# DMA row length of the first load in a streaming row-sum kernel

## The chip, the cores and the metric

The kernel runs on one core of a Trainium2 chip. The metric is device time in microseconds of one execution.

## The reference

```python
# x: (32, 512, 1024) float32, multiplier: 0.5
def reference(x, multiplier):
    return (np.sum(x, axis=-1) * multiplier).astype(np.float32)
```

There are 16384 rows of 1024 numbers, 67.1 MB to read and 65.5 KB to write. Each number is used once.

## The kernel before

The 16384 rows are cut into eight blocks of 128 partitions x 16 rows. Seven blocks are whole loads of 8.39 MB into three rotating buffers; in HBM, the 16 rows of one partition lie one after another, so a partition's part of a block is one run of 64 KiB. The vector engine (DVE) sums each block with one instruction; of block 6 the scalar engine (ACT) takes half. The last block comes in five pieces, so that little work is left when the last byte has landed.

```python
    x_pool = ctx.enter_context(tc.tile_pool(name="x", bufs=3))
    # ... cut ...
    for b in range(n_blocks - 1):
        c0 = b * B                                   # B = 16
        t = x_pool.tile([P, B, D], fp32, name="xb")  # 128 x 16 x 1024
        loads.append(nc.sync.dma_start(out=t, in_=x_rows[:, c0 : c0 + B, :]))
        h = B if b < n_blocks - 2 else B // 2
        nc.vector.reduce_sum(
            out=sums[:, c0 : c0 + h], in_=t[:, 0:h, :], axis=mybir.AxisListType.X
        )
        # ... multiply by 0.5 into res; half of block 6 goes to the scalar engine ...
    # ... last block: loads of 8, 5 and 2 rows, then the last row in two parts ...
    # ... two stores of the results ...
    # at build time, loads that wait for nothing are moved to the program's entry
```

## Time and profile before

| what | before | where from |
|---|---|---|
| time | 162.17 us (161.99 to 162.18) | three runs |
| span of the profiled run | 160.2 us | page, first line |
| DMA packets | 2016, 97.4% of 16 engines' span | page, part 3 |
| DVE busy | 74% | page, part 1 |
| first block seen by DVE | 21.78 us | timeline |
| one further whole load | 19.33 to 19.35 us | distance between the starts of two reductions |

"Seen" is the moment at which DVE begins on a block, some 0.02 us after the last of the 16 engines has reported its part landed. A load is spread over 16 DMA engines, and each moves 8 partitions of it. Since DVE starts each block only when it has landed, the distance between two starts is the time that the DMA engines took for one load. The lines themselves stand in the prediction below.

### The profile page before, as it was taken

What the parts mean: (1) busy time and instruction counts of PE and PEld (TensorE: products, weight loads), DVE (VectorE), ACT (ScalarE), POOL (GpSimd) and SP (SyncE); (2) the same over time, 40 slices, a digit from 0 to 9 for tenths busy, and PEclk for the clock granted to TensorE, in tenths of its full rate; (3) what the DMA queues carried; (4) which work ended last, traced back from release to release, by engine and by line L of the source; (5) the groups of instructions that cost most, each with busy time, mean ns of one, the idle gap of its engine ahead of it and who ended that gap; (6) DMA issues with size and microseconds to landing.
All of it is one profiled execution on the core that took longest, in us unless ns stands there. A gap on an engine that the chain in (4) does not pass through costs nothing.

```text
span 160.2 us, 138 instructions
## 1 busy us (share of the span) xinstructions
DVE 119.3 (74%) x34; ACT 17.3 (11%) x31; POOL 0.2 (0%) x4
## 2 busy tenths in 40 slices
DVE  0000059997799969999599995999959999597443
ACT  0000000000000000000000000000000000599952
POOL 0000000000000000000000000000000000000000
DMA  7996996996996996997997998979969969999992
GB/s 278 507 524 262 524 524 262 524 524 262 524 524 262 524 524 262 524 475 311 524 442 344 524 409 376 524 311 475 524 278 507 524 278 507 393 393 425 430 399 72
DMA packets 2016, 67.18 MB, mean 419 GB/s; under 512 B 480, under 2 KB 608, under 8 KB 736
## 3 DMA queue, kind: packets, MB, share of 16 engines
q1 hardware_dynamic: 2016, 67.18, 97.4%
HBM read 67.11 MB, written 0.07 MB: 419 GB/s over the span
## 4 chain that ended last, share of the span: by engine, by line
DMA 75%; DVE 22%; SPq 1%; issue 0%; DVEq 0%
DMA xb<-in_x_dram 75%; DVE sums L96 22%; SPq L114 1%; DVE xb L80 0%; SPq L120 0%; SPq L94 0%; DVE res L99 0%; DVEq L205 0%
## 5 line engine op out<-in xcount | busy, mean ns | idle before, releaser
L96 DVE TENSOR_REDUCE sums<-xb 128x16 f32<-128x16384 f32 (+1 forms) x7 | 112.0, 16001 | 33.3 <-DMA xb<-in_x_dram 33.3
L70 ACT ACT_TABLE_LOAD x1 | 1.3, 1283 | 137.9 <-DMA xb<-in_x_dram 137.9
L70 ACT ACTIVATE xb<-xb 128x1024 f32<-128x1024 f32 x15 | 15.7, 1045 | 2.1 <-DMA xb<-in_x_dram 2.1
L80 DVE CUSTOM_DVE_ANT_0 xb<-xb 128x512 f32<-128x512 f32 (+1 forms) x9 | 5.6, 664 | 5.0 <-DMA xb<-in_x_dram 5.0
L70 ACT ACTIVATION_READ_ACCUMULATOR xb<-xb 128x1 f32 x15 | 2.8, 187 | 0.0
L99 DVE TENSOR_SCALAR res<-sums 128x16 f32<-128x16 f32 (+1 forms) x7 | 1.2, 174 | 0.2
L80 DVE DVE_READ_ACCUMULATOR2_ANT res<- 128x1 f32 x9 | 0.7, 83 | 0.0
L80 DVE CUSTOM_DVE_ANT_0 xb<-xb,part 128x224 f32<-128x224 f32 x1 | 0.5, 450 | 0.2 <-DMA xb<-in_x_dram 0.2
L191 POOL MEMSET const-bfloat16-1.0<- 128x1 bf16 x1 | 0.1, 101 | 0.0
L191 POOL MEMSET const-uint8-127<- 128x1 uint8 x1 | 0.1, 101 | 0.0
L191 POOL MEMSET const-float32-0.0<- 128x1 f32 x1 | 0.1, 98 | 0.2 <-issue 0.2
L191 POOL MEMSET const-float32-1.0<- 128x1 f32 x1 | 0.1, 98 | 0.0
L80 DVE DVE_READ_ACCUMULATOR2_ANT part<- 128x1 f32 x1 | 0.1, 83 | 0.0
## 6 DMA issues: line engine op xcount, KB each, us to landing
xb<-in_x_dram SPq DMA_DIRECT2D x1, 4096.0 KB, 31.1
xb<-in_x_dram SPq DMA_DIRECT2D x1, 2560.0 KB, 36.9
xb<-in_x_dram SPq DMA_DIRECT2D x1, 1024.0 KB, 38.9
xb<-in_x_dram SPq DMA_DIRECT2D x1, 288.0 KB, 39.1
xb<-in_x_dram SPq DMA_DIRECT2D x1, 224.0 KB, 39.2
xb<-in_x_dram SPq DMA_DIRECT2D x7, 40.8
out_dram<-res SPq DMA_DIRECT2D x1, 56.0 KB, 10.0
out_dram<-res SPq DMA_DIRECT2D x1, 8.0 KB, 1.4
```

The costliest lines, as they stand in the source:

```text
L70: acts.append(nc.scalar.activation(out=t[:, r, :], in_=t[:, r, :], func=mybir.ActivationFunctionType.Copy, scale=mul, accum_out=res[:, col ...
L80: return nc.vector.tensor_tensor_reduce(out=t[:, r, lo:mid], in0=t[:, r, lo:mid], in1=t[:, r, mid:hi], scale=mul, scalar=start, op0=ADD, o ...
L96: nc.vector.reduce_sum(out=sums[:, c0 : c0 + h], in_=t[:, 0:h, :], axis=mybir.AxisListType.X)
L99: nc.vector.tensor_single_scalar(out=res[:, c0 : c0 + h], in_=sums[:, c0 : c0 + h], scalar=mul, op=mybir.AluOpType.mult,)
L114: nc.sync.dma_start(out=t[:, lo:hi, :], in_=x_last[:, lo:hi, :])
L191: nc = _bacc.Bacc("TRN2", target_bir_lowering=False, num_devices=1)
```

## The change

A DMA is cut into packets of one contiguous run each, here 64 KiB at most. The change caps the run at 8 KiB for the first block alone, so that its 128 packets become 1024. Its intent is to have the first, cold load run in shorter units, so that all engines come up to speed sooner; bytes, addresses, buffers and order stay.

```diff
-        loads.append(nc.sync.dma_start(out=t, in_=x_rows[:, c0 : c0 + B, :]))
+        loads.append(
+            nc.sync.dma_start(
+                out=t,
+                in_=x_rows[:, c0 : c0 + B, :],
+                max_dma_last_dim=65536 if b else 8192,
+            )
+        )
```

The first load's pattern goes from 128 x 16384 elements to 128 x 8 x 2048, one dimension more. Nothing else differs.

## The prediction

> **What bounds the kernel now.** I read the first page for the load of each engine and of the DMA queue, then the chain of waits in order of time, then the timeline for the moments at which each load was seen, and last a table of stretches cut at exactly those moments. The page and the chain first:
>
> ```profile
> DVE 119.3 (74%) x34; ACT 17.3 (11%) x31; POOL 0.2 (0%) x4
> q1 hardware_dynamic: 2016, 67.18, 97.4%
> DMA 75%; DVE 22%; SPq 1%; issue 0%; DVEq 0%
> ```
>
> The reader is to see one queue whose packets fill 97.4% of the time of 16 DMA engines, beside a vector engine (DVE) that is busy 74%. The chain puts 22% on DVE, and that needs care. It gets there because a load into one of three buffers waits for the reduction that frees the buffer. Here is where it does so (start, length, what):
>
> ```profile
> 0.43 40.66 DMA xb<-in_x_dram
> 41.09 0.02 issue
> 41.11 17.23 DVE sums L96
> 58.34 0.02 issue
> 58.36 40.78 DMA xb<-in_x_dram
> ```
>
> A load issued at 58.36 us takes 40.78 us to land because an earlier load is still draining in front of it in the queue. One whole load takes about 19.3 us, so the queue holds work for some 21 us when the buffer comes free: the link through DVE has that much slack, and the true chain is the queue alone. The table of stretches tests this. Its columns are the stretch, its length, busy time of each engine, the clock, the mean share of the DMA engines and GB/s:
>
> ```profile
> 0.00:21.78 21.78, 0.00 (x1) 0.00 (x0) 0.20 (x4) 1.00 1.02 433
> 21.78:41.11 19.33, 17.39 (x2) 0.00 (x0) 0.00 (x0) 1.00 1.00 434
> 41.11:137.87 96.76, 86.98 (x11) 0.00 (x0) 0.00 (x0) 1.00 0.99 428
> 137.87:147.58 9.71, 8.86 (x3) 9.64 (x17) 0.00 (x0) 1.00 0.97 418
> 147.58:153.68 6.10, 2.54 (x8) 4.34 (x9) 0.00 (x0) 1.00 0.99 424
> 153.68:156.18 2.50, 1.93 (x7) 2.19 (x5) 0.00 (x0) 1.00 0.97 398
> ```
>
> Each edge is the moment at which a consumer starts on a freshly landed load, so each length is the time of one load (the third: of five). From 21.78 us on, the DMA share is 0.97 to 1.00, and the rate is flat at about 430 GB/s. The kernel is bound by the DMA engines' own rate from about 2 us to about 157.5 us. DVE has 1.9 us idle ahead of each block, as the timeline says of the second:
>
> ```profile
> 21.78 17.22 DVE L96 TENSOR_REDUCE sums<-xb 128x16 f32<-128x16384 f32 x1 [21.78 <-DMA xb<-in_x_dram]
> 41.11 17.22 DVE L96 TENSOR_REDUCE sums<-xb 128x16 f32<-128x16384 f32 x1 [1.91 <-DMA xb<-in_x_dram]
> ```
>
> So whatever delays the DMA engines anywhere delays the end by the same amount. Nothing later in the queue absorbs it.
>
> **What the Trainium skill says.** (1) "DMA: Bandwidth & Descriptors", section "Where 436 GB/s comes from", gives a ceiling of 435.2 GB/s for the 16 ports. The 434 GB/s of a whole 64 KiB-row load says that it is reached: no row size can make a load appreciably faster. (2) The same page, "Why small descriptors are slow (HBM only)", names a fixed cost for each packet of about 3 cycles inside the DMA engine, and a fetch of 32 bytes of descriptor data. Three cycles at the 850 MHz of section (1) would be 3.5 ns. The trace agrees that there is a fixed cost but shows a larger one, 10 to 12 ns with all that goes with it (below); I use the trace's. (3) The same page, "Why a DMA increments its semaphore by 16 and not by 1": the number of engines is set by the slowest dimension. It is 128 partitions before and after, so all 16 engines stay in use, with an eighth of the partitions' bytes each. The trace before moves 434 GB/s, which needs all 16. (4) "Perfetto Trace Analysis", section "DMA Instruction — HWDGE (DVE, Sync)": an engine may begin to consume descriptors before all of them have been generated. No view of the kernel before can show this for 1024 descriptors, since all of its DMAs have 128 data packets each.
>
> **The change part by part.** Bytes, addresses, buffers, waits and the order of instructions stay as they are; only the first load is cut into 128 x 8 packets of 8 KiB where it had 128 of 64 KiB.
>
> Removed: 128 packets of 64 KiB, 8 for each engine. One takes 19.33 / 8 = 2.416 us.
>
> Added: 1024 packets of 8 KiB, 64 for each engine. The kernel already has loads with shorter rows, and each is also 8 packets for each engine. The stretches of its last block give their cost: 32 KiB rows (8 rows of x) 9.71 / 8 = 1.214 us, 20 KiB rows 6.10 / 8 = 0.763 us, 8 KiB rows 2.50 / 8 = 0.3125 us. At the 64 KiB rate they would be 1.208, 0.755 and 0.302. The excess of a packet over a share of a long one is therefore (2 x 1.214 - 2.416) / 1 = 12 ns from the first, (3.2 x 0.763 - 2.416) / 2.2 = 11 ns from the second, (8 x 0.3125 - 2.416) / 7 = 12 ns from the third. It contains the completion packets of these loads, of which the changed load has no more than before, and edges read to 0.01 us, so I take 8 to 11 ns. Each engine gets 64 - 8 = 56 more packets: 56 x 8 to 11 ns = 0.45 to 0.62 us, middle 0.53 us. All of it lies on the path.
>
> Start-up, the uncertain term: the first load is seen at 21.78 us, of which 8 x 2.416 = 19.33 us is transfer at full rate and 2.45 us is start. In the window of the first 3.2 us of the trace, the 16 first packets (one for each engine) have a share of 90.0%:
>
> ```profile
> DMA packets 16, 1.05 MB, mean 328 GB/s; under 512 B 0, under 2 KB 0, under 8 KB 0
> q1 hardware_dynamic: 16, 1.05, 90.0%
> ```
>
> That is 0.900 x 3.2 = 2.88 us for each packet, 0.46 us more than later ones. Shorter packets could cut this, or move it. Against that stands the making of eight times as many descriptors. The closing store bounds its speed: all 144 of its packets (128 and 16 completions) begin within 5 slices of 0.055 us, 0.275 us, so at most 1.9 ns for each. The new load needs 1024 + 16: at most 2.0 us. If they are made engine by engine, the last engine could begin up to 15/16 of 2.0 = 1.9 us after the first; today's first packets are spread over about 0.9 us (slices of the first 3 us). The worst case of this step is thus an estimate of +1.0 us; if engines are served in turn or the present 0.9 us has another cause that overlaps, 0. I put +0.1 us on start-up as a whole, between -0.4 and +1.0.
>
> Moved: the first reduction starts 0.5 to 0.6 us later, so the fourth load is issued that much later, still about 20 us before the queue would run dry. DVE's, ACT's and the store's work doesn't change. The issuing queue may take longer over the first instruction (0.38 us now); the second load has some 20 us to be ready, so this is hidden.
>
> Sum: 0.53 + 0.1 = +0.6 us; 162.17 + 0.6 = about 162.8, which I shade to **162.7 us** since the packet cost is more likely at its lower end.
>
> **The rivals.**
> *A faster start.* Packets of 8 KiB let writes finish earlier and might recover the 0.46 us stretch of the first packets. For it: the stretch is real. Against it: the last engine to start sets when the load is complete, and a stretch caused by 16 engines beginning at once on cold memory wouldn't ask for the packet size. It would make about 162.2 us, a net of nothing.
> *Descriptors become the bound.* If the generator is slower with three-dimensional patterns, or stops when one engine's ring is full and leaves the others unfed, the engines start one after another; 16 steps of 0.3 us would add 5 us: 167 us. Against it: 144 packets within 0.275 us at the end. For it: nothing in this trace has more than 9 packets for each engine in one DMA.
> *Hidden anyway.* If DVE were the bound after the first block, a late first block would cost nothing. Against it: 1.91 us idle before each block and a DMA share of 0.99 to 1.00. I give it no weight.
> *Better interleaving.* Desynchronised engines could raise the rate of later loads. Against it: 434 of 435.2 GB/s leaves nothing.
>
> **Range and chances.** Low is the packet cost at 0.45 us with 0.4 us won at start and the spread of the three runs (162.0). High is 0.62 + 0.8 us (163.6). Two per cent are 3.2 us: for faster there is no store of time that large in reach, 1%; slower needs the second rival, 4%; within 2%, 95%.
>
> **What would show it.** In the changed profile: 896 packets more (2016 to 2912); the first reduction at about 22.3 us, against 21.78; after that the same 19.33 us between blocks, and the end shifted by what the first block lost; a packet's mean in the first 20 us at about 310 ns. If the first reduction moves by less than 0.3 us, the start-up won; if by more than 1.2 us, the descriptors were late, and the first packets' starts would be spread wider than 0.9 us. If the intervals of later blocks change, I was wrong that only the first load is touched.

## The result, and the profile after

The changed kernel took 162.68 us (162.57 to 162.80, four runs), against 162.10 us for the kernel before on the same chip: 0.58 us more. The ratio is 1.0036, with a 95% interval of 1.0021 to 1.0051. (Ratios here are the mean time of one kernel's fast runs over that of the other's in the same rounds, so they are not quite the ratio of the medians.) Within 2% this is the same time, but the 0.58 us are real.

The page of the changed kernel, first its DVE line and then the DMA queue; the span in the first line of that page is 160.8 us:

```profile
DVE 119.3 (74%) x34; ACT 17.3 (11%) x31; POOL 0.2 (0%) x4
q1 hardware_dynamic: 2912, 67.18, 97.6%
```

There are 896 packets more, as 1024 - 128 requires. No engine has other work. The table of stretches of the changed kernel, cut again at the starts of consumers (columns: stretch, length, busy time of DVE, ACT and GpSimd (POOL), clock, mean DMA share, GB/s):

```profile
0.00:22.39 22.39, 0.00 (x0) 0.00 (x0) 0.20 (x4) 1.00 1.03 421
22.39:41.74 19.35, 17.39 (x2) 0.00 (x0) 0.00 (x0) 1.00 1.00 434
41.74:138.50 96.76, 86.98 (x11) 0.00 (x0) 0.00 (x0) 1.00 0.99 428
138.50:148.21 9.71, 8.86 (x2) 9.64 (x17) 0.00 (x0) 1.00 0.98 422
148.21:154.31 6.10, 2.55 (x9) 4.36 (x10) 0.00 (x0) 1.00 0.98 418
```

The reader is to compare the lengths with those of before. The first stretch grew from 21.78 to 22.39 us, by 0.61 us. Every other length is the same to 0.02 us. (Single packets are booked in the stretch in which they begin, so shares can pass 1.) What the first block lost is what the end lost: the later blocks neither add to it nor absorb it. The idle time of DVE ahead of each later block is unchanged too:

```profile
22.39 17.22 DVE L102 TENSOR_REDUCE sums<-xb 128x16 f32<-128x16384 f32 x1 [22.39 <-DMA xb<-in_x_dram]
41.74 17.22 DVE L102 TENSOR_REDUCE sums<-xb 128x16 f32<-128x16384 f32 x1 [1.92 <-DMA xb<-in_x_dram]
```

### The profile page after: what moved, and what is told of

It is laid out like the page before. It is cut to its first block, busy times and chain, and to the rows that moved or that the text cites. A ratio compares the mean times of both kernels' runs of the same rounds, so it can differ in the third digit from the quotient of the medians.

```text
span 160.8 us, 138 instructions
## 1 busy us (share of the span) xinstructions
DVE 119.3 (74%) x34; ACT 17.3 (11%) x31; POOL 0.2 (0%) x4
## 4 chain that ended last, share of the span: by engine, by line
DMA 75%; DVE 22%; SPq 1%; issue 0%; DVEq 0%
DMA xb<-in_x_dram 75%; DVE sums L102 21%; SPq L120 1%; DVE xb L80 0%; SPq L95 0%; SPq L126 0%; DVE res L105 0%; DVEq L211 0%
```

## The experiments

The prediction had put 0.53 us on the packets themselves and 0.1 us on start-up. The trace after seemed to contradict this split. In its packet records, the first 30 or so 8 KiB packets of an engine begin 306 ns apart, only 4 ns more than an eighth of a 64 KiB packet's 2.416 us, and from about the fortieth on 310 ns apart. Summed over 56 extra packets this gave some 0.38 us, and left 0.2 us for start-up. So there were three theories: **A**, packets 0.38 us and start-up 0.2 us; **B**, all of it packets, 10.7 ns each (the texts add "as the prediction had it", but the prediction's own split is 9.5 ns and 0.1 us of start-up); **C**, all of it the cold start, in which case short rows would be free later on. They part where short rows are moved away from the start. All edits below are against the changed kernel unless said otherwise. All results were correct.

### The same short rows in mid-stream (mid8k)

```diff
-                max_dma_last_dim=65536 if b else 8192,
+                max_dma_last_dim=8192 if b == 3 else 65536,
```

> Only the fourth block has rows of 8 KiB, so the same 56 extra packets per engine flow in mid-stream and the start is that of the kernel before. Theory A (two terms: packets cost about 0.38 us for 56 extra wherever they are, the cold start costs another 0.2 us): +0.3 to +0.4 us, this load takes 19.7 us where the others take 19.35. Theory B (all of the 0.6 us is packets, 10.7 ns each, as the prediction had it): +0.6 us, this load 19.95 us. Theory C (all of it is start-up, packets are free): 0.

Measured: 162.65 us against 162.10, +0.55 us; ratio 1.0033 (1.0021 to 1.0046). The stretches of this run's trace:

```profile
0.00:21.81 21.81, 0.00 (x0) 0.00 (x0) 0.20 (x4) 1.00 1.03 433
21.81:41.16 19.35, 17.39 (x2) 0.00 (x0) 0.00 (x0) 1.00 1.00 434
41.16:60.52 19.36, 17.39 (x2) 0.00 (x0) 0.00 (x0) 1.00 0.92 398
60.52:80.40 19.88, 17.40 (x3) 0.00 (x0) 0.00 (x0) 1.00 1.08 457
80.40:99.75 19.35, 17.39 (x2) 0.00 (x0) 0.00 (x0) 1.00 1.00 434
```

The block with short rows takes 19.88 us where its neighbours take 19.35 or 19.36: 0.53 us, or 9.5 ns for each of the 56 extra packets, with no cold start in it. Theory C falls, and A's 19.7 us is missed by 0.2. Theory B's sum of 0.6 us is met by the total within noise; its load of 19.95 us was a little too long.

Why did the packet records mislead? The gap between an engine's last packet record and its completion arriving is 0.35 us (mean of the 16 engines) for the three loads ahead of the short rows here, 0.47 us for the load with short rows, and stays at 0.47 us for the loads after it. So 0.12 us of the cost is not in the records of the packets but in a lag behind them, which grows while short packets run and then stands still. (Long packets move it too, more slowly: in the kernel before it goes from 0.35 us at the first load to 0.40 us at the fifth.) That it is one side of the engine running ahead of the other until some buffer is full would fit, and would fit the change from 306 to 310 ns; it is an inference, and no run here shows the buffer. The landings count, and they say 19.88 us.

### Short rows in all seven whole blocks (all8k)

```diff
-                max_dma_last_dim=65536 if b else 8192,
+                max_dma_last_dim=8192,
```

> All seven whole blocks in rows of 8 KiB. Theory A: 7 x 0.38 + 0.2 = +2.9 us. Theory B: 7 x 0.6 = +4.2 us. Theory C: +0.6 us. If the 310 ns spacing of the later packets (306 at first) is the true rate of a long stream, each later load takes 19.85 us and the sum is 7 x 0.5 = +3.5 us.

Measured: 165.87 us, +3.77 us; ratio 1.0232 (1.0216 to 1.0248). The trace:

```profile
0.00:22.53 22.53, 0.00 (x0) 0.00 (x0) 0.20 (x4) 1.00 0.96 391
22.53:42.41 19.88, 17.39 (x2) 0.00 (x0) 0.00 (x0) 1.00 1.01 422
42.41:121.94 79.53, 69.58 (x8) 0.00 (x0) 0.00 (x0) 1.00 1.01 422
```

The third stretch holds four loads: 79.53 / 4 = 19.88 us each. Seven times 0.53 us is 3.71 us, and about 0.06 us is left for the start. That is the "+3.5 us" variant of what was expected, a little exceeded; the others are excluded, B's too, since its 10.7 ns for a packet was too dear. The prediction's own 9.5 ns fits. From exact landing times (means over the 16 engines) a short-row load takes 19.879 us and a long-row one 19.350, so one packet costs 0.529 / 56 = **9.4 ns**.

This run also shows a stall that costs nothing. The timeline of the queue that issues the loads (SPq, that of the sync engine; start, length of all three issues together):

```profile
0.00 19.11 SPq L95 DMA_DIRECT2D xb<-in_x_dram  x3
```

In the kernel before, the first three issues are through after 1.33 us. Here the third alone stood for 18.0 us, from 1.1 to 19.1 us. That so many descriptors found no room yet would fit; the trace does not show what it waited for. The DMA share from 3 us to the end of this stall is 1.01, as in the changed kernel, so the DMA engines did not starve.

### Shorter and longer rows in the first block (first4k, first32k, first2k)

```diff
-                max_dma_last_dim=65536 if b else 8192,
+                max_dma_last_dim=65536 if b else 4096,     # first4k
+                max_dma_last_dim=65536 if b else 32768,    # first32k
+                max_dma_last_dim=65536 if b else 2048,     # first2k
```

> First block in rows of 4 KiB: 120 extra packets per engine. Theory A with a start-up term that doesn't depend on the number: 120 x 6.8 ns + 0.2 = +1.0 us. Theory A with a start-up term that grows with the descriptors to be made: 0.8 + 0.4 = +1.2 us. Theory B: 120 x 10.7 = +1.3 us. Theory C with a constant start: +0.6 us.

> First block in rows of 32 KiB: 8 extra packets per engine. Theory A: 0.05 us of packets; a start-up term that comes from short or many packets would be nearly gone, +0.1 us in all; if it comes from the three-dimensional pattern itself, +0.25 us. Theory B: +0.09 us.

> First block in rows of 2 KiB: 248 extra packets per engine. Linear theory (each extra packet 9.4 ns, from the seven loads of all8k, and 0.1 us of start): 2.33 + 0.1 = +2.4 us. Rival (making descriptors becomes the bound, or the queue runs full and starves engines, since the issue of later loads already stood still for 9 to 18 us with 4 KiB rows and with 8 KiB rows everywhere): clearly more, +4 us or over.

| rows of first block | extra packets for each engine | time, us | over before, us | 9.4 ns x packets, us |
|---|---|---|---|---|
| 64 KiB | 0 | 162.10 | | |
| 32 KiB | 8 | 162.31 | +0.21 | 0.08 |
| 8 KiB | 56 | 162.68 | +0.58 | 0.53 |
| 4 KiB | 120 | 163.27 | +1.17 | 1.13 |
| 2 KiB | 248 | 164.41 | +2.30 | 2.33 |

The time follows the number of packets in a straight line from 32 KiB to 2 KiB, within 0.13 us. For 4 KiB rows the measured +1.17 is next to what A with a growing start had asked for (+1.2), between A with a constant start (+1.0) and B (+1.3), so that run alone tells less than it was sent for; its start-up, read below, did not grow. For 2 KiB the rival was that the making of 4096 descriptors becomes the bound; it asked for +4 us or more, and falls, although the second issue stood still for 14.7 us there. The DMA view of that run between 5 and 20 us:

```profile
DMA packets 2846, 5.83 MB, mean 389 GB/s; under 512 B 0, under 2 KB 0, under 8 KB 2846
```

The rate is still 389 GB/s with rows of 2 KiB, against 434 with 64 KiB and 422 with 8 KiB.

The 32 KiB run is 0.21 us late at the median (ratio 1.0011, interval 0.9998 to 1.0023, so not clear of zero). The median is more than its eight packets explain, and near the +0.25 us that was expected if the three-dimensional pattern itself costs start-up.

### 32 KiB rows in mid-stream, one look (mid32k)

```diff
-                max_dma_last_dim=65536 if b else 8192,
+                max_dma_last_dim=32768 if b == 3 else 65536,
```

> Fourth block alone in rows of 32 KiB: 8 extra packets per engine. Linear theory: its load takes 19.35 + 8 x 9.4 ns = 19.43 us. First32k was seen 0.1 to 0.16 us late; if this one is only 0.08 late, the rest there was start-up.

```profile
41.24:60.60 19.36, 17.39 (x2) 0.00 (x0) 0.00 (x0) 1.00 0.94 406
60.60:80.02 19.42, 17.39 (x2) 0.00 (x0) 0.00 (x0) 1.00 1.06 459
80.02:99.38 19.36, 17.39 (x2) 0.00 (x0) 0.00 (x0) 1.00 1.00 433
```

The load with 32 KiB rows took 19.42 us between neighbours of 19.36: 0.06 us for eight packets, or 0.08 us by the mean landings, about what the line says. If first32k's 0.21 us is real, part of it is not packets and belongs to the start.

### The same 1024 packets in eight loads (pieces8)

This one is an edit of the kernel before. The first block's 8 KiB runs are issued as eight loads of 128 packets, each in the plain two-dimensional pattern.

```diff
-        loads.append(nc.sync.dma_start(out=t, in_=x_rows[:, c0 : c0 + B, :]))
+        step = B if b else 2
+        for r in range(0, B, step):
+            loads.append(
+                nc.sync.dma_start(
+                    out=t[:, r : r + step, :],
+                    in_=x_rows[:, c0 + r : c0 + r + step, :],
+                )
+            )
```

> First block in the same 1024 packets of 8 KiB, but issued as eight loads of 128 packets each, in the plain pattern. If only the number of packets counts: 56 x 9.4 ns = +0.53 us, and up to 0.07 us for seven more completions per engine, +0.5 to +0.6 us. If 1024 descriptors in one load are what costs: about +0.1 us. If the first instruction's pattern costs start-up: the first issue takes 0.38 us again, not 0.44.

Measured: 162.45 us against 162.11, +0.34 us; ratio 1.0021 (1.0008 to 1.0034, that is +0.1 to +0.55 us). That is lower than was expected, and 0.23 us below the changed kernel. By the mean landings in its trace, the eight pieces land 2.485 us apart, the eighth 17.392 us after the first. One piece at the full rate is 2.409 us (1.05 MB at 435.2 GB/s, an estimate from the ceiling that the prediction cites from the Trainium skill, "DMA: Bandwidth & Descriptors", section "Where 436 GB/s comes from"); with 8 x 9.4 ns that is 2.485 us. So the packets cost the same in small loads as in one large one, and seven more completions for each engine cost nothing that shows. The first issue took 0.376 us again. The packets alone ask for +0.53 us, and the median shows 0.19 us less; the upper end of the interval just reaches it. In the traces the last load of input lands 0.47 us later than before, in this run as in mid8k, so the difference may be noise of single executions; it stays open.

### The changed kernel once more (after_again)

No edit.

> The changed kernel once more beside these, for the size of the start-up term: 162.65 to 162.75 us, +0.6 us; the first issue 0.43 us again, the first reduction at 22.3 to 22.5 us.

Measured: 162.68 us against 162.11; ratio 1.0036 (1.0023 to 1.0049). The result repeats to 0.01 us. This allows start-up to be read by subtraction. From the mean landing time of the first block I take 19.275 us (its bytes at 435.2 GB/s, the same estimate) and 9.4 ns for each packet:

| first block's pattern | runs | start-up, us |
|---|---|---|
| two-dimensional, 64 KiB rows (and pieces8) | before, mid8k, mid32k, pieces8 | 2.21, 2.13, 2.17, 2.16; mean 2.17 |
| three-dimensional, 32 to 2 KiB rows | first32k, the change twice, all8k, first4k, first2k | 2.26, 2.27, 2.27, 2.32, 2.24, 2.18; mean 2.26 |

The three-dimensional pattern starts 0.09 us later, whether it has 2 or 32 packets for each partition. Some 0.05 us of it can be seen in the first issue itself, which took 0.37 to 0.38 us in the four runs of the first line and 0.42 to 0.44 us in the six of the second. The first packet of any engine begins at 0.99 to 1.04 us in the four and at 1.06 to 1.11 us in the six, 0.08 us later on average: a direct reading that needs no subtraction. The chain of waits of the changed kernel begins so:

```profile
0.00 0.44 SPq L95
0.44 0.05 issue
0.49 41.24 DMA xb<-in_x_dram
```

In the kernel before, the same first piece is 0.38 us long:

```profile
0.00 0.38 SPq L94
0.38 0.05 issue
```

The two groups of the table spread by about 0.1 us each and overlap a little (2.21 and 2.18), so the 0.09 us is good to some 0.05; the times of the first packets do not overlap. With one trace for each run this is a small effect on ten executions, and what the queue does in the longer issue isn't shown.

## Why the prediction was right

**The bound and the missing slack.** The prediction said that the DMA engines' rate binds from 2 to 157.5 us and that a delay anywhere reaches the end in full. The first block became 0.61 us later, every further interval kept its length, and the time grew by 0.58 us. In mid8k the delay came from the fourth block and also passed through (0.53 and 0.55 us).

**The packets.** Predicted: 8 to 11 ns for each extra packet, 0.45 to 0.62 us, read off the shorter loads of the last block. Measured: 9.4 ns and 0.53 us, from mid8k and all8k. Reading the cost from landings was the right way; my own later reading from packet records was 0.15 us too low, and mid8k showed it. But the exact figure owes something to luck. The prediction's three readings were 12, 11 and 12 ns, which is 0.6 to 0.7 us, and it lowered them to 8 to 11 because those loads also have completions. In pieces8 more completions cost nothing that shows. The readings were high for another reason: they were differences of edges read to 0.01 us, set against 19.33 us, the shortest of the intervals. By mean landings in the same trace, against 19.352 us, the three loads give about 10, 9 and 11 ns.

**Start-up.** Predicted: +0.1 us between -0.4 and +1.0. Measured: +0.09 us. That the two agree is luck, since the prediction named no mechanism of this size. The one that the runs show it had written off: it expected a longer first issue to be hidden, because the second load has some 20 us to be ready. But the first load waits for that issue too, which took 0.42 to 0.44 us in place of 0.37 to 0.38, and its packets began 0.08 us later. The mechanisms named for the wide range both failed to appear. The first packets of the engines began within 0.3 us of each other (1.10 to 1.42 us) where they had been spread over 0.9 us, so descriptors were not late. Nor is that narrower spread the change's doing: in mid8k, whose first block has 64 KiB rows, it is 0.3 us as well, and in mid32k 0.65 us. And nothing was won: the first block's bytes were not moving sooner. By the packet records, the first eighth of the load's bytes had been moved at 4.42 us after the change and at 4.30 us before.

**The rivals.** A faster start would have made 162.2 us and did not happen. Descriptors as the bound asked for 167 us; even 4096 of them (first2k) cost only the packets' line. Hidden anyway asked for no change and falls with mid8k. Better interleaving asked for shorter later intervals; they are 19.35 us as before.

**The sum.** 162.7 us was forecast and 162.68 us measured. Its large term, the packets, was right in place and in size. That it agrees to 0.02 us is luck: the sum was 162.8 before it was shaded, and the kernel before is 162.10 us on more runs where the prediction had 162.17. Two slips did not move the forecast: each engine has a sixteenth of the partitions and not "an eighth", and the upper end of the range counted 0.8 us of start-up where the step itself allowed 1.0. The mark that the prediction set for a packet's mean, about 310 ns in the first 20 us, is met: the DMA view of the changed kernel from 3 to 20.5 us has

```profile
DMA packets 910, 7.45 MB, mean 426 GB/s; under 512 B 0, under 2 KB 0, under 8 KB 0
q1 hardware_dynamic: 910, 7.45, 101.2%
```

which is 1.012 x 17.5 us x 16 / 910 = 311 ns.

## What to carry to other kernels

When the DMA queue never runs dry, count packets for each engine: here each one more cost about 9.4 ns, whether in the first load or a later one and in one large load or several small ones, so the longest contiguous rows, here 64 KiB, were the best, and above 8 KiB there is under 3% left to win. Read such a cost from the times at which loads land, not from the spacing of packet records, which hid a fifth of it. A cold start that looks stretched in the first packets was not made shorter by shorter packets here.

## What the Trainium skill lacked or had wrong

- "DMA: Bandwidth & Descriptors", section "Why small descriptors are slow (HBM only)": it names about 3 cycles for each packet (3.5 ns at 850 MHz, an estimate) and a fetch of 32 bytes. The runs show 9.4 ns for each packet in all, the same to about 10% for rows from 2 KiB to 8 KiB.
- The same page has a rate for loads that the sync engine issues on trn2 at one row length only (4 KiB, in its section on iDMA), and no series. The runs show 434 GB/s for 64 KiB rows, 422 for 8 KiB and 389 for 2 KiB, on one core alone.
- "Perfetto Trace Analysis", section "DMA Instruction — HWDGE (DVE, Sync)", says that engines may begin before all descriptors are made, if more are made than fit, and its table lets the issue last until all are made. It doesn't say how long that can be, nor whether it costs anything: an issue took 18.0 us in all8k, 14.7 us in first2k and 9.0 us in first4k, against 0.43 us, with the DMA engines fully fed.
- No page has the cost of one more dimension in a load's pattern: the first issue took 0.42 to 0.44 us in place of 0.37 to 0.38, and the first packet began 0.08 us later.
- No page says that the gap between an engine's last packet record and the landing can change: it went from 0.35 to 0.47 us over one load of short rows and stayed there.
